# The first FFN's LayerNorm: three of its eight quarters turned by DMA, and the product behind it taken by pairs of K tiles

## The chip, the cores and the metric

One core of a Trainium2 chip runs the whole kernel in one launch. The metric is device time in microseconds; 2433.03 is the median of three runs of the kernel before (2432.76 to 2437.99).

## The reference

One layer of a streaming encoder over 256 tokens of width 2048, in float32, post-norm with `ALPHA = 2 ** 0.25`:

```python
h = layer_norm(ALPHA * h + 0.5 * swiglu_ffn(h, ffn1_w_in, ffn1_w_out), ln_ffn1_g, ln_ffn1_b)
mix = hybrid_mixer(h, w_in, ...)          # A: chunked attention, B: latent attention, both gated
h = layer_norm(ALPHA * h + mix, ...)
h = layer_norm(ALPHA * h + memory_cross_attention(h, mem, ...), ...)
h = layer_norm(ALPHA * h + 0.5 * swiglu_ffn(h, ...), ...)
# in hybrid_mixer: qa, ka, va, q_lat, kv_lat, gates = split(u @ w_in)
```

The change lies between the first `layer_norm` and the products `va` (2048 x 1024, the values of attention A) and `gates`.

## The kernel before

Weights stream from memory in blocks of 128 x 2048 (1 MB): K on the partitions, 16 K tiles of 128. Every float32 operand is split in two rounded halves, hi and lo, and a product is three matmuls: hi·hi, lo·hi and hi·lo. For weights `halves` (L258 to L268) does the split: two casts on ScalarE (L264) and one subtraction on VectorE (L267). Three raw buffers hold loaded blocks, two pairs of buffers ("units") hold the split ones; a block with tags goes to other, named buffers instead. SyncE issues the loads in order (L193); a load waits until the subtraction has released its raw buffer.

The activations are held transposed (`T`, four blocks of four K tiles, each with hi and lo for both tiles of 128 tokens). A LayerNorm therefore ends with a turning. `ln_T` (L405 to L434) takes quarters of 512 columns: it normalises one (even quarters on VectorE L413, odd ones on ScalarE L415), turns its four 128 x 128 tiles on TensorE into PSUM (L421, placed behind the last matmul in program order), applies gain and bias alternately on ScalarE (L428) and VectorE (L430), and splits the result (`split`, L254 to L257). The scale comes from `ln_scale`, a chain of some ten small VectorE operations whose last one is `self.chain`; the low halves of weights are queued behind that one.

The FFN's last output product and the next product are *skewed*: four weight blocks are kept, the first token tile goes through all four, then the second, so that a LayerNorm's turning can run beside the other tile's matmuls. Behind the FFN comes `mixer` (L869). Its first product, A's values, takes `w_va` in eight blocks of four K tiles by 512 columns: the first column half skewed over both token tiles, all 16 K tiles each, then the second half for both tiles together (`mm_tok`, L298). Into it are woven the second token tile's LayerNorm, and in its second half four `forms_step`, sums of activation tiles that the gates' products need (L321, L325). Each value result is copied from PSUM by L891. Behind it stand four gate products (`pair_group`: `mm_pair`, L311, and a seven-product scheme over sums of weights, `mm_sums`, L366), the latent product and the projections.

A scheduler orders the instructions of each engine ahead of time: by program order, moved forward by a priority (`SOON` is 400), as they become ready in its own model. `issue_after(x)` forces an instruction behind `x` on its engine.

The other way of turning exists already, for the LayerNorm before cross-attention (`turned_norm`, L1386): a quarter is normalised on VectorE (L1405), its 32-bit words are copied on ScalarE into two planes of 16 bits (L846), a transposing DMA from SyncE turns them (L850), ScalarE joins the planes again (L854), gain and bias follow from SBUF (L1426, L1428), then the split.

Of the kernel before, what the change touches and what calls it, by code (L numbers as in the profile page):

```python
# [101 lines left out]
class Kernel:  # L102
    def __init__(self, ctx, tc, t, out):
        self.tc, self.nc, self.t, self.out = tc, tc.nc, t, out

        def pool(name, bufs=1, **kw):
            return ctx.enter_context(tc.tile_pool(name=name, bufs=bufs, **kw))

        self.const = pool("const")
        self.wraw = pool("wraw", 3)  # L110
        self.whi = pool("whi", UNITS)
        self.wlo = pool("wlo", UNITS)
        self.blocks = pool("blocks")
# [8 lines left out]
        self.cut = self.early = False  # L122


# [46 lines left out]
    def weave(self, main, side, prio=SOON):  # L171

        for i in range(len(main) + 1):
            for f in side.get(i, ()):
                self.add(f, prio=prio, held=main[i][2] if i < len(main) else 0)
            if i < len(main):
                self.items.append(main[i])

    def run(self):
# [21 lines left out]
        def load(i):  # L201
# [3 lines left out]
            if isinstance(w, Sums):  # L205
                n = 4 * w.m
                got = self.halves(raw[:, w.m:n], *self.unit()), self.halves(
                    sums[i][:, :n], *(self.block(g, (P, 2048), F32R) for g in w.tags))
            else:
                ap, tags = w  # L210
                hi, lo = (self.block(g, (P, 2048), F32R) for g in tags[:2]) if tags else self.unit()
                first = {"turned": self.ln_act, "next": self.last_hi}.get(tags[2]) if tags and len(tags) > 2 else None
                with self.tc.issue_after(first.ins) if first else nullcontext():
                    got = self.halves(raw[:, :ap.shape[1]], hi, lo)
            form_sums(i + 1)
# [38 lines left out]
    def split(self, src, hi, lo):  # L254
        copied = self.nc.scalar.copy(hi, src)
        self.nc.vector.tensor_tensor(lo, src, hi.bitcast(F32), ALU.subtract)
        return copied  # L257

    def halves(self, src, hi, lo):

# [41 lines left out]

    def mm_pair(self, ps, w, n, x, kts, first, last):

        for wi in range(2):
            for j, kt in enumerate(kts):
                for tt in range(2):
                    for g in range(2):
# [97 lines left out]
    def ln_T(self, h, mr, tt, ln, xT, qs=range(4)):  # L406
# [3 lines left out]
        for q in qs:  # L410
# [349 lines left out]
    def out_proj(self, wname, nk, x, scale, st, steps=None, tags=None, n0=0, other=False, cut=False):  # L760
# [109 lines left out]
    def mixer(self, xT, st, steps):  # L870
# [4 lines left out]

        va, kept, ps1 = {}, {}, {}

        def val(n, tts, g, ps, tags=None, held=0, keep=False, again=False):
            def fn(w=None):
                if keep:  # L880
                    kept[g] = w
                w = kept.pop(g) if again else w
                for tt in tts:
                    if g == 0:
                        ps[tt] = self.mm_tile()
                    self.mm_tok(ps[tt], tt, w, xT(), range(4 * g, 4 * g + 4), g == 0, g == 3)
                if g == 3:
                    if "t" not in va:
                        va["t"] = self.block("H4", (P, 2, 1024))
                    for tt in tts:  # L890
                        (nc.vector.tensor_copy if tt else nc.scalar.copy)(  # L891
                            va["t"][:, tt, n * 512:(n + 1) * 512], ps[tt])
            ap = t["w_va"][n, :, g * 2048:(g + 1) * 2048]
            self.add(fn, *(() if again else ((ap, tags),)), held=held)

        ps = {}
        first = self.collect(lambda: self.skewed(
            lambda tt, g, **kw: val(0, (tt,), g, ps, **kw), (),
            (None, None, ("H5", "H0", "early"), ("X0", "X1", "turned"))))
        a, b, c = steps(1)  # L900
        self.weave(first, {0: a, 3: b, 4: c})
        gates, fx = {}, {}
        second = self.collect(lambda: [val(1, (0, 1), g, ps1) for g in range(4)])
        self.weave(second, {1 + i: [self.forms_step(fx, SUMS_GATE, c, xT)] for i, c in enumerate(SUMS_GATE)}, prio=0)


# [7 lines left out]
        def gate(n):  # L914
            ps, qs = {}, {}

            def product():
# [7 lines left out]
                if n < 2:  # L925
                    load_bias(n + 2)
            self.pair_group(n % 2, t["w_gate"][n], 512, KT, xT, AT_GATE[n], fx, ps, qs, None, SUM_HOME + ("H5",),
                            ORDER_GATE if len(AT_GATE[n]) > 3 else None)
# [53 lines left out]

        self.pair_group(0, t["w_lat"][0], 512, KT, xT, SUMS_IN, fx, lps, lqs, None, SUM_HOME + ("H5",))
        self.add(lat_scale, prio=SOON)
# [7 lines left out]
        def kpe(w):  # L992
# [3 lines left out]
            rope = self.rotation()  # L996
            ps = self.at_tile()
            for kt in range(KT):
# [386 lines left out]

    def turned_norm(self, ln, st, x):  # L1386

# [4 lines left out]
        def scale(tt):  # L1392
            def fn():
                if tt == 0:
                    x["T"] = self.act(["T0", "T1", "T2", "T3"])
                got[tt] = self.ln_scale(st[tt])
            return fn

        def planes(tt, q):
            def fn():  # L1400
                if tt == 0:
                    e[q] = self.block(("X2", "X3", "H5", "H4")[q], (P, 2, 2, 512))
# [14 lines left out]
        def join(tt, q):  # L1417
            def fn():
# [222 lines left out]
    def build(self):  # L1641
# [57 lines left out]
def _layout(i):  # L1699
# [22 lines left out]
    r["w_qk"] = np.stack([_feat(w[:, :aw]), _feat(w[:, aw:2 * aw])], 1)  # L1722
    r["w_va"] = _tok(w[:, 2 * aw:3 * aw])
    c = 3 * aw
# [52 lines left out]
```

## Time and profile before

| | |
|---|---|
| runs, median (lowest to highest) | 2433.03 us (2432.76 to 2437.99) |
| profiled execution, its span | 2432.52 us, 2430.7 us |
| TensorE busy | 2422.3 us, 11280 matmuls |
| VectorE busy | 2130.9 us |
| ScalarE busy | 1553.2 us |
| granted TensorE clock | 1.00 throughout |

Busy shares are of the span. Matmuls overlap in the record, so a row's length is a little over the distance from its start to the next row's start; distances between starts are the measure used. Times in rows count from the start of the span. The stretch of the change is 677 to 730 us: the FFN's last two blocks for the second token tile, the LayerNorm's turnings, A's values.

### The profile page before, as it was taken

How to read it: one execution, taken by the hardware profiler on the slowest of the kernel's cores; microseconds unless marked ns; L12 is line 12 of the kernel's file. 1: busy time of each engine (PE TensorE's matmuls, PEld its weight loads, DVE VectorE, ACT ScalarE, POOL GpSimd, SP SyncE). 2: the span in 40 equal slices, each digit the busy share in tenths (PEclk: the TensorE clock that was granted, in tenths of full speed). 3: DMA queues.
4: the chain of work that ended last, by engine and by line, in shares of the span. 5: the costliest groups of instructions: out<-in, count | busy, mean ns of one | idle time of the engine just before them, and what ended most of it. 6: DMA issues, size and time to landing. Idle time of an engine off the chain costs nothing.

```text
span 2430.7 us, 29702 instructions
## 1 busy us (share of the span) xinstructions
PE 2422.3 (100%) x11280; PEld 2022.8 (83%) x11280; DVE 2130.9 (88%) x2437; ACT 1553.2 (64%) x2022; POOL 35.9 (1%) x81
## 2 busy tenths in 40 slices
PE   9999999999999999999999999999999999999999
PEld 8888888888888888888888888888888888888887
DVE  8999989899889998779788889979879999888997
ACT  6676745666555557878565687765666675556662
POOL 0000000000000001000000000000000000000000
PEclk9999999999999999999999999999999999999999
DMA  7766656667656657776577577655556766666665
GB/s 268 252 212 214 207 200 222 210 201 219 224 176 215 216 195 248 229 210 176 183 246 256 167 241 213 220 181 192 190 199 214 229 221 210 220 207 207 200 220 182
DMA packets 176414, 516.20 MB, mean 212 GB/s; under 512 B 111728, under 2 KB 112496, under 8 KB 121104
## 3 DMA queue, kind: packets, MB, share of 16 engines
q1 hardware_dynamic: 170816, 495.83, 61.6%
q0 software_dynamic: 4592, 17.30, 2.2%
q8 instruction: 88, 1.44, 0.2%
q10 hardware_dynamic: 864, 1.18, 0.1%
q14 instruction: 54, 0.44, 0.1%
HBM read 485.30 MB, written 2.10 MB: 201 GB/s over the span
## 4 chain that ended last, share of the span: by engine, by line
PE 89%; DVE 4%; ACT 3%; DMA 1%; issue 1%; SPq 0%; DVEq 0%; ACTq 0%
PE at L311 24%; PE mm L311 23%; PE at L366 11%; PE mm L366 11%; PE mm L298 10%; PE mm L277 4%; PE mm L279 2%; DVE lo L267 2%; ACT hi L264 1%; PE at L1034 1%; PE at L1505 0%; PE at L277 0%; DMA raw<-w_xv 0%; PE at L1088 0%; ACT H L854 0%
## 5 line engine op out<-in xcount | busy, mean ns | idle before, releaser
L264 ACT CAST hi<-raw 128x1024 fp32r<-128x1024 f32 (+1 forms) x852 | 804.0, 981 | 458.0 <-PE at L311 150.1
L267 DVE TENSOR_TENSOR lo<-raw,hi 128x2048 fp32r<-128x2048 f32 (+1 forms) x427 | 902.0, 2114 | 134.8 <-ACT hi L264 129.0
L311 PE MATMUL mm<-hi,T 128*128 128x512 f32 (+1 forms) x1312 | 307.5, 384 | 0.8 <-DVE v L400 0.7
L311 PEld LDWEIGHTS mm<-hi,T 128*128 128x128 f32 x1312 | 244.5, 188 | 46.9 <-DVE v L400 1.1
L264 ACT CAST X<-H 128x1024 fp32r<-128x1024 f32 (+1 forms) x170 | 174.8, 1035 | 160.9 <-DVE H L248 119.9
L311 PE MATMUL at<-hi,T 128*128 128x512 f32 x1136 | 272.3, 390 | 0.0
L311 PEld LDWEIGHTS at<-hi,T 128*128 128x128 f32 x1136 | 213.3, 188 | 44.5
L267 DVE TENSOR_TENSOR X<-H,X 128x2048 fp32r<-128x2048 f32 (+1 forms) x85 | 191.4, 2252 | 64.7 <-ACT X L264 64.7
L311 PE MATMUL mm<-lo,T 128*128 128x512 f32 (+1 forms) x656 | 158.4, 383 | 0.0
L311 PE MATMUL at<-lo,T 128*128 128x512 f32 x568 | 141.0, 389 | 0.0
L311 PEld LDWEIGHTS mm<-lo,T 128*128 128x128 f32 x656 | 122.3, 188 | 22.4
L311 PE MATMUL at<-hi,H 128*128 128x512 f32 x560 | 133.8, 390 | 0.0
L311 PEld LDWEIGHTS at<-lo,T 128*128 128x128 f32 x568 | 106.7, 188 | 22.1
L311 PEld LDWEIGHTS at<-hi,H 128*128 128x128 f32 x560 | 105.0, 188 | 21.5
L250 DVE TENSOR_TENSOR H<-H,raw 128x512 f32<-128x512 f32 (+1 forms) x170 | 115.4, 679 | 2.2
L311 PE MATMUL mm<-hi,H 128*128 128x512 f32 x480 | 115.5, 392 | 0.1
L311 PEld LDWEIGHTS mm<-hi,H 128*128 128x128 f32 x480 | 89.6, 188 | 18.9 <-DVE w L684 0.5
L248 DVE TENSOR_TENSOR H<-raw 128x1024 f32<-128x1024 f32 (+1 forms) x85 | 102.1, 1201 | 0.6 <-DMA raw<-w_gate 0.4
L366 PE MATMUL mm<-X,X 128*128 128x512 f32 x342 | 91.4, 393 | 0.0
L264 ACT CAST X<-raw 128x1024 fp32r<-128x1024 f32 (+1 forms) x54 | 55.4, 1035 | 47.9 <-DVE raw L250 38.6
L366 PE MATMUL at<-X,X 128*128 128x512 f32 (+1 forms) x315 | 82.6, 386 | 0.7 <-ACT X L264 0.7
L854 ACT COPY w<-w 128x1024 uint16<-128x1024 uint16 (+1 forms) x60 | 75.7, 1275 | 1.4 <-DMA w<-w 1.4
(387 smaller groups left out, 4151.3 us busy)
## 6 DMA issues: line engine op xcount, KB each, us to landing
raw<-ffn_w_in SPq DMA_DIRECT2D x150, 1024.0 KB, 4.9
raw<-ffn_w_out SPq DMA_DIRECT2D x66, 1024.0 KB, 4.9
raw<-w_gate SPq DMA_DIRECT2D x32, 1024.0 KB, 4.8
raw<-ffn_w_out_r SPq DMA_DIRECT2D x16, 1024.0 KB, 4.9
raw<-w_qk SPq DMA_DIRECT2D x16, 1024.0 KB, 5.6
raw<-w_o_b SPq DMA_DIRECT2D x16, 1024.0 KB, 4.8
raw<-w_out SPq DMA_DIRECT2D x16, 1024.0 KB, 5.0
raw<-w_xk SPq DMA_DIRECT2D x16, 1024.0 KB, 5.4
```

The lines of the kernel that those rows point to most:

```text
L248: self.nc.vector.tensor_tensor(two[0], two[1], raw[:, :m].unsqueeze(1).to_broadcast([P, 2, m]), ALU.add)
L250: self.nc.vector.tensor_tensor(t[:, a * m:a * m + m], t[:, b * m:b * m + m], raw[:, a * m:a * m + m], ALU.add)
L264: self.last_hi = self.nc.scalar.copy(hi[:, c:d], src[:, c:d])
L267: self.last_lo = self.nc.vector.tensor_tensor(lo[:, :n], src, hi[:, :n].bitcast(F32), ALU.subtract)
L277: self.nc.tensor.matmul(ps, hi[j], x.both(kt), start=(j == 0), stop=False)
L279: self.last_mm = self.nc.tensor.matmul(ps[:, :S], lo[j], x.at(0, kt), start=False, stop=(j == n - 1))
L298: self.last_mm = self.nc.tensor.matmul(ps, x.at(xi, kt)[:, tt * P:(tt + 1) * P], w[wi][:, j * 512 + c:j * 512 + c + m], start=(start and j ...
L311: self.last_mm = self.nc.tensor.matmul(ps[tt, g][:, :n], x.at(xi, kt)[:, tt * P:(tt + 1) * P], w[wi][:, c:c + n], start=first and j + wi + ...
L366: self.last_mm = self.nc.tensor.matmul(bank[:, :m], a[xi], v[wi][:, c * m:(c + 1) * m], start=own and first and wi + xi == 0, stop=own and ...
L854: self.nc.scalar.copy(self.words(u, n).rearrange("p (c k) -> p k c", k=2), self.words(s, n).rearrange("p (k c) -> p k c", k=2))
L1034: nc.tensor.matmul(ps[:, c0:c0 + nk], q[:, tt * P:(tt + 1) * P], k[:, :nk], start=(j == 0), stop=(j == len(parts) - 1))
```

## The change

- For the first FFN's LayerNorm, quarters 2 and 3 of the first token tile and quarter 3 of the second are turned by DMA; the other five stay on TensorE. Their normalising is queued behind the last low half of a turned quarter (`ln_lo`), their planes copy behind its rounding (`ln_act`). The planes stand in buffers `F` and `X2`.
- A's values take `w_va` in pairs of K tiles by both column halves, into four PSUM banks: K tiles 0 to 7 skewed (first tile, then second), K tiles 8 to 15 for both tiles together. The layout in memory follows.
- The low half of the third value block (tag "after") is not queued behind the scale's chain but after the first tile's turned quarters.
- The four `forms_step` and the copies of the values stand at the end of the product; the gates', the latent and the rotary key's products exchange the PSUM banks they use.

```diff
     def ln_T(...):
             turned = self.split(v, hi, lo)
-            if q == 1:
-                self.ln_act = turned
+            if q == qs[-1]:
+                self.ln_act, self.ln_lo = turned, self.last_split
+        while self.late:
+            self.late.pop(0)(self.ln_lo)
...
-    def halves(self, src, hi, lo):
+    def halves(self, src, hi, lo, late=False):
...
-        with self.tc.issue_after(self.chain.ins) if self.chain is not None else nullcontext():
-            self.last_lo = self.nc.vector.tensor_tensor(lo[:, :n], src, hi[:, :n].bitcast(F32), ALU.subtract)
+        def low(behind=None):
+            first = behind or self.chain
+            with self.tc.issue_after(first.ins) if first is not None else nullcontext():
+                self.last_lo = self.nc.vector.tensor_tensor(lo[:, :n], src, hi[:, :n].bitcast(F32), ALU.subtract)
+        if late:
+            self.late.append(low)
+        else:
+            low()
...
+    def skewed_pairs(self, src, ps, xT, side, tags):
+        kept = {}
+        def add(k, tts, tags=None, held=0, keep=False, again=False):
+            def fn(w=None):
+                if keep:
+                    kept[k] = w
+                w = kept.pop(k) if again else w
+                if k == 0:
+                    ps.update({(tt, g): self.group_tile(0) for tt in tts for g in range(2)})
+                self.mm_pair(ps, w, 512, xT(), (2 * k, 2 * k + 1), k == 0, k == 7, tts)
+            self.add(fn, *(() if again else ((src[:, k * 2048:(k + 1) * 2048], tags),)), held=held)
+        def build():
+            self.skewed(lambda tt, k, **kw: add(k, (tt,), **kw), (), tags)
+            for k in range(4, 8):
+                add(k, (0, 1))
+        self.weave(self.collect(build), side)
...
     def mixer(self, xT, st, steps):
+        side = dict(steps(1))
+        for i, c in enumerate(SUMS_GATE):
+            side.setdefault(9 + i, []).append((self.forms_step(fx, SUMS_GATE, c, xT), 0))
+        side[12].insert(0, values)
+        self.skewed_pairs(t["w_va"][0], ps, xT, side, (None, None, ("H5", "H0", "early", "after"), ("X0", "X1", "turned")))
...
-            self.pair_group(n % 2, t["w_gate"][n], ...)
+            self.pair_group(n % 2 ^ 1, t["w_gate"][n], ...)
...
     def planes(tt, q):                      # in turned_norm
-                nc.vector.tensor_scalar(hs, hs, mean, r, ALU.subtract, ALU.mult)
-                with self.tc.issue_after(self.next_hi.ins):
+                with nullcontext() if homes[0] else self.tc.issue_after(self.ln_lo.ins):
+                    nc.vector.tensor_scalar(hs, hs, mean, r, ALU.subtract, ALU.mult)
+                with self.tc.issue_after((self.next_hi if homes[0] else self.ln_act).ins):
                     self.planes(hs, e[q][:, tt, 0, :], 512)
...
+        if not homes[0]:
+            def low(f, *a):
+                return f(*a), 0
+            side = {0: [scale(1)], 1: [low(planes, 0, 2), low(planes, 0, 3)], 2: [low(send, 0, 2)],
+                    3: [low(send, 0, 3), near(1)], 5: [near(1, (2,)), low(planes, 1, 3)],
+                    6: [low(join, 0, 2), low(send, 1, 3)], 7: [low(join, 0, 3)], 9: [low(join, 1, 3)]}
+            return lambda tt: side if tt else ([scale(0)], [near(0)], [])
...
-        ln = [self.ln_steps(n, st, x) for n in ("ln_ffn1", "ln_mix", "ln_x")]
+        ln = [self.turned_norm("ln_ffn1", st, x, (None, None, "F", "X2")), None, self.ln_steps("ln_x", st, x)]
```

The keys of `side` are places in the product of A's values: 0 to 3 are the first tile's K tile pairs 0 to 3, 4 to 7 the second tile's, 8 to 11 the pairs 4 to 7 for both.

## Rows read from the trace of the kernel before

**Rows 1.** The page: busy us, share of the span and instructions of each engine.

```profile
PE 2422.3 (100%) x11280; PEld 2022.8 (83%) x11280; DVE 2130.9 (88%) x2437; ACT 1553.2 (64%) x2022; POOL 35.9 (1%) x81
```

**Rows 2.** Stretches: start and end, length, busy us of each engine, granted clock, DMA.

```profile
677.40:729.70 52.30, 52.30 (x247) 43.24 (x246) 44.48 (x88) 31.85 (x52) 1.23 (x2) 1.00 0.43 150
...
707.90:729.70 21.80, 21.80 (x98) 18.03 (x97) 16.84 (x24) 11.03 (x16) 1.23 (x2) 1.00 0.61 212
729.70:771.00 41.30, 41.30 (x184) 34.23 (x183) 36.35 (x30) 23.74 (x28) 0.00 (x0) 1.00 0.63 225
```

**Rows 3.** Waits of PE: line, releaser, us in total, times, longest.

```profile
PE at L493 <- DVE w L470: 1.1, 1, 1.1
```

**Rows 4.** Timeline of PE: start, us, line, operation, out<-in, count.

```profile
677.41 2.88 PE L298 MATMUL mm<-X,H 128*128 128x512 f32 x12
680.27 1.06 PE L421 MATMUL at<-ident,h 128*128 128x128 f32 x8
681.09 2.32 PE L298 MATMUL mm<-X,H 128*128 128x512 f32 x9
683.25 1.03 PE L421 MATMUL at<-ident,h 128*128 128x128 f32 x8
684.04 2.28 PE L298 MATMUL mm<-hi,T 128*128 128x512 f32 x8
...
693.31 3.01 PE L298 MATMUL mm<-X,T 128*128 128x512 f32 x12
...
707.93 1.98 PE L298 MATMUL mm<-hi,T 128*128 128x512 f32 x8
...
729.69 3.79 PE L311 MATMUL mm<-hi,T 128*128 128x512 f32 x16
```

**Rows 5.** Timeline of DVE, same columns; in brackets idle time before and its releaser.

```profile
675.01 2.27 DVE L267 TENSOR_TENSOR H<-raw,H 128x2048 fp32r<-128x2048 f32 x1
677.20 0.26 DVE L395 BATCH_NORM_AGGREGATE mv<-bn 128x2 f32<-128x24 f32 x1
...
683.68 0.69 DVE L256 TENSOR_TENSOR T<-w,T 128x512 fp32r<-128x512 f32 x1 [0.34 <-ACT T L255]
...
707.89 0.29 DVE L325 TENSOR_TENSOR w<-w 128x128 f32<-128x128 f32 x1
...
727.78 2.28 DVE L267 TENSOR_TENSOR X<-H,X 128x2048 fp32r<-128x2048 f32 x1
```

**Rows 6.** Timeline of ACT.

```profile
701.07 2.96 ACT L264 CAST hi<-raw 128x1024 fp32r<-128x1024 f32 x3
```

**Rows 7.** Timeline of SP, the loads of w_va.

```profile
673.80 0.33 SPq L193 DMA_DIRECT2D raw<-w_va  x1
...
677.32 0.33 SPq L193 DMA_DIRECT2D raw<-w_va  x1
...
693.78 0.33 SPq L193 DMA_DIRECT2D raw<-w_va  x1
```

**Rows 8.** Instructions on tile H, 1375 to 1440 us: ns min/median/max, first, last start.

```profile
L1426 ACT ACTIVATE H<-H,vecs x8: 478/493/513, 1420.6 to 1433.7; 128x128 f32<-128x128 f32 x8
L846 ACT COPY H<-h x4: 1042/1060/1063, 1399.2 to 1417.2; 128x1024 uint16<-128x1024 uint16 x4
...
L854 ACT COPY H<-H x4: 1346/1354/1381, 1418.2 to 1428.9; 128x1024 uint16<-128x1024 uint16 x4
L255 ACT CAST T<-H x4: 609/614/638, 1421.6 to 1435.0; 128x512 fp32r<-128x512 f32 x4
...
DMA to landing us min/median/max: 3.0/3.5/4.2
```

**Rows 9.** Line L850, all transposing DMAs.

```profile
DMA to landing us min/median/max: 2.7/3.2/12.9
```

**Rows 10.** Timeline of PE beside the turnings before cross-attention.

```profile
1396.18 3.92 PE L277 MATMUL mm<-H,hi 128*128 128x512 f32 x16 [0.28 <-ACT hi L264]
```

**Rows 11.** Chain that ended last, 1375 to 1440 us: start, us, what.

```profile
1389.39 5.67 DMA raw<-w_xk
```

More of the change, by code (lines that the diff above doesn't have):

```diff
@@ L122, in __init__ @@
         self.cut = self.early = False
+        self.late = []
     def name(self, s):
@@ L174, in weave @@
             for f in side.get(i, ()):
-                self.add(f, prio=prio, held=main[i][2] if i < len(main) else 0)
+                f, p = f if isinstance(f, tuple) else (f, prio)
+                self.add(f, prio=p, held=main[i][2] if i < len(main) else 0)
             if i < len(main):
@@ L213, in load @@
                 with self.tc.issue_after(first.ins) if first else nullcontext():
-                    got = self.halves(raw[:, :ap.shape[1]], hi, lo)
+                    got = self.halves(raw[:, :ap.shape[1]], hi, lo, bool(tags) and "after" in tags)
             form_sums(i + 1)
@@ L301, in mm_tok, with mm_pair @@
                     )
-    def mm_pair(self, ps, w, n, x, kts, first, last):
+    def mm_pair(self, ps, w, n, x, kts, first, last, tts=(0, 1)):
         for wi in range(2):
             for j, kt in enumerate(kts):
-                for tt in range(2):
+                for tt in tts:
                     for g in range(2):
@@ L873, in mixer, with values @@
         e = self.__dict__
[L876 to L904, printed above, removed]
+        va, ps, gates, fx = {}, {}, {}, {}
+        def values():
+            va["t"] = self.block("H4", (P, 2, 1024))
+            for n in range(2):
+                for tt in range(2):
+                    (nc.vector.tensor_copy if tt else nc.scalar.copy)(
+                        va["t"][:, tt, n * 512:(n + 1) * 512], ps[tt, n])
+        side = dict(steps(1))
[3 more added lines that the diff above has]
+        self.skewed_pairs(t["w_va"][0], ps, xT, side, (None, None, ("H5", "H0", "early", "after"), ("X0", "X1", "turned")))
         bias = {}
@@ L926, in product @@
                     load_bias(n + 2)
-            self.pair_group(n % 2, t["w_gate"][n], 512, KT, xT, AT_GATE[n], fx, ps, qs, None, SUM_HOME + ("H5",),
+            self.pair_group(n % 2 ^ 1, t["w_gate"][n], 512, KT, xT, AT_GATE[n], fx, ps, qs, None, SUM_HOME + ("H5",),
                             ORDER_GATE if len(AT_GATE[n]) > 3 else None)
@@ L981, in lat_join @@
             return fn
-        self.pair_group(0, t["w_lat"][0], 512, KT, xT, SUMS_IN, fx, lps, lqs, None, SUM_HOME + ("H5",))
+        self.pair_group(1, t["w_lat"][0], 512, KT, xT, SUMS_IN, fx, lps, lqs, None, SUM_HOME + ("H5",))
         self.add(lat_scale, prio=SOON)
@@ L996, in kpe @@
             rope = self.rotation()
-            ps = self.at_tile()
+            ps = self.mm_tile()
             for kt in range(KT):
@@ L1384, in mem_norm, with turned_norm @@
         return {0: [load], 2: [stat(0)], 6: [stat(1)], 8: [spread], 9: [quarter(0)], 11: [quarter(1)], 13: [quarter(2)], 14: [quarter(3)]}
-    def turned_norm(self, ln, st, x):
+    def turned_norm(self, ln, st, x, homes=("X2", "X3", "H5", "H4")):
         nc, e, got = self.nc, {}, {}
@@ L1393, in fn @@
             def fn():
-                if tt == 0:
+                if tt == 0 and homes[0]:
                     x["T"] = self.act(["T0", "T1", "T2", "T3"])
@@ L1397, in scale, with near, fn @@
             return fn
+        def near(tt, qs=(0, 1)):
+            def fn():
+                if tt == 0:
+                    x["T"] = self.act(["T0", "T1", "T2", "T3"])
+                self.ln_T(self.h[tt], got[tt], tt, ln, x["T"], qs)
+            return fn
         def planes(tt, q):
             def fn():
-                if tt == 0:
-                    e[q] = self.block(("X2", "X3", "H5", "H4")[q], (P, 2, 2, 512))
+                if q not in e:
+                    e[q] = self.block(homes[q], (P, 2, 2, 512))
                 mean, r, nb = got[tt]
                 hs = self.h[tt][:, q * 512:(q + 1) * 512]
-                nc.vector.tensor_scalar(hs, hs, mean, r, ALU.subtract, ALU.mult)
-                with self.tc.issue_after(self.next_hi.ins):
+                with nullcontext() if homes[0] else self.tc.issue_after(self.ln_lo.ins):
+                    nc.vector.tensor_scalar(hs, hs, mean, r, ALU.subtract, ALU.mult)
+                with self.tc.issue_after((self.next_hi if homes[0] else self.ln_act).ins):
                     self.planes(hs, e[q][:, tt, 0, :], 512)
@@ L1722, in _layout @@
     r["w_qk"] = np.stack([_feat(w[:, :aw]), _feat(w[:, aw:2 * aw])], 1)
-    r["w_va"] = _tok(w[:, 2 * aw:3 * aw])
+    r["w_va"] = _pairs(*_halves(w[:, 2 * aw:3 * aw]), 512, [()])
     c = 3 * aw
```

2 lines of the change are left out of this document (1 added, 1 removed).

## The prediction

> **What bounds it.** Read in this order: the busy shares, the stretch of the change, TensorE's waits, then the engines' timelines around the first FFN's LayerNorm. TensorE is busy 2422.3 of 2430.7 us [rows 1], in the changed stretch 52.30 of 52.30 at a granted clock of 1.00, which is 2.4 GHz [rows 2]; its longest wait for another engine in the whole span is 1.1 us, at the start [rows 3]. So the time is a sum of matmuls, and a change can win only what it takes off TensorE and the small gaps between its instructions. The reader is to see this in the timeline: from 707.93 to 729.69 stand 96 matmuls of 512 columns, 0.2267 us each, without a gap [rows 4]. VectorE is second, 44.48 of 52.30 us here and 36.35 of 41.30 in the first gate group behind it [rows 2].
>
> **What leaves TensorE.** Eight turnings take from 680.27 to 681.09 and from 683.25 to 684.04: 0.82 and 0.79 us, 0.10 each [rows 4]. Three of eight quarters at four turnings each no longer run there: 12 x 0.10 = 1.2 us. The product A's values keeps its 192 matmuls (16 K tiles x 3 passes x 2 token tiles x 2 column halves, in another order).
>
> **Entries.** The 12 matmuls from 677.41 end at 680.13, the turnings start at 680.27; the nine from 681.09 end at 683.13, the next start at 683.25: about 0.13 us a group [rows 4]. Four groups become three (two of eight, one of four): 0.13 us.
>
> **The low half out of the chain.** VectorE rounds `lo` of the third weight block from 675.01 for 2.27 us, and the aggregate of the first token tile starts behind it at 677.20 [rows 5]. Moved behind the turned quarters, it lets the chain of small operations start about 2.1 us earlier. The turnings still stand behind TensorE's matmuls, which end at 680.13, so only the 0.14 us of waiting before the first of them can go. The price is that this raw buffer comes free later: the load at 677.32 is the one it releases [rows 7]. The casts of this block and the one before it run only from 701.07 on [rows 6], so some 10 us of slack (a load at 688, landed by 695) hide it.
>
> **Cover lost.** Today eight turnings of the second half stand between the last FFN matmuls and the first value matmuls, while the first quarter is evacuated, scaled and split. Its low half is written at 683.68 + 0.69 = 684.37 [rows 5], 4.1 us after the turnings began; even so the first eight value matmuls took 2.28 us against 1.98 in later rows, 0.3 us of waiting [rows 4]. Afterwards TensorE reaches them at 680.13 + 0.80 + 9 x 0.2267 = 682.97 and wants the first low half 0.23 later, at 683.2. At today's pace it would come at 680.13 + 4.1 = 684.2, a wait of 1.0; if ScalarE, which has one normalisation less in front, and the earlier chain bring it 0.7 sooner, 0.3. I take 0.7, nearest to the row's own pace, 0.4 more than today. For the second token tile 12 matmuls (2.72) still stand behind the turnings, as at 693.31 [rows 4], so 3.5 us cover a chain of some 3.8: 0.05 more than today.
>
> **Sum.** -1.2 - 0.13 - 0.14 + 0.4 + 0.05 = -1.0 us. The profiled execution took 2432.52 us (span 2430.7, 1.8 around it); the median of the runs is 2433.03, 0.5 above. Against the median: 2432.0 us.
>
> **What is added beside TensorE.** Each turned quarter has on ScalarE a planes copy of 1.06 us, a joining copy of 1.35 and two scalings of 0.49, and on SyncE a transposing DMA landing 3.5 us after its issue, 4.2 at most here [rows 8], 12.9 at most anywhere [rows 9]. Three times the two copies is 7.2 us more ScalarE work, less the PSUM reads that were there anyway; ScalarE is busy 31.85 of 52.30 [rows 2], so I cost it at nothing while it is in time. VectorE normalises the odd quarters too, about 1 us more.
>
> Whether it is in time is the open cost. First token tile, third quarter: ordered behind the low half of quarter two (about 685), then perhaps behind the postponed 2.27, so normalised by about 688, copied to planes by 689, landed by about 693. The join then stands on ScalarE behind the next weight's cast, which needs a high buffer that TensorE frees only after the second tile's first eight matmuls, about 698: the cast of 2.0 us ends near 701. The join and what follows it (1.35 + 2 x 0.49 + 0.61 [rows 8] + 0.69 [rows 5] = 3.6) end at 704.6 if the join goes next. TensorE wants it where it takes up both tiles at once, which is 707.93 today [rows 4] and about 706.9 after. A margin of 2.3 us: cost 0. If two casts of the following weight (2.0) and the last quarter's planes (1.06) go before the join, it is 707.7: 0.8 late. With the slow landing 12.9 nothing changes until the landing passes 701. Ends: 0 and about +5; I take 0 because the nearest rows, the same kind of turning before cross-attention, show one wait of 0.28 us [rows 10].
>
> The four sum forms move from beside the second half of the values to behind it: each a sum and a split of 0.69 us and four of 0.29 [rows 5], 2.5 us of VectorE, 10 in all, some 6 us of it now later than today, in a stretch with 21.80 - 16.84 = 5 us free [rows 2]. What doesn't fit slides into the first gate, whose first summed weight is rounded at 727.78 for 2.28 and used at 737 to 739, 7 to 9 us of slack [rows 5]. Cost 0, ends 0 and +3. The exchange of PSUM banks only swaps which four are in use; the four values copies must end within the 5.44 us of the first gate pair. Cost 0.
>
> **A rule that speaks against it.** By rows a turned tile costs TensorE 0.10 us, and by DMA some 7 us of latency over three engines [rows 4, 8]. The Trainium skill, "VectorE: DVE Perf Modes", section "Rules for kernel authors", says of a 128x128 transpose: "Use TensorE if PSUM dest is OK; xbar DMA otherwise". Its section "The three transpose paths" gives 390 ns against 1309 (bf16); by those figures the move would lose, which is what the first rival makes of it. On a TensorE that is always busy the row's 0.10 us is what counts.
>
> **Rivals.**
> 1. A turned quarter comes late (slower than before). Place: the first matmul on K tiles 8 and 9, or 12 and 13 for the last quarter, which is planed only near 704, landed at 709, and joined at 713.5 against a need at 717. Price: the wait itself, 1 to 5 us; it decides from 1.0 us of waiting on. At 2.5 us: 2434.5. For it: ScalarE has in the 9 us before that place two pairs of casts (4.0), a planes copy (1.06), the second tile's third quarter (1.5) and the first join (2.9), 9.5 in all; against it: the margins above.
> 2. VectorE's backlog reaches the gates: forms and joins (+5 us of work) against 5 us free; a wait of 1.5 us: 2433.5. Against it: 7 to 9 us of slack.
> 3. Weight loads queue behind the DMA turnings on SyncE. Today the fifth block is loaded at 673.80 and the seventh at 693.78 [rows 7]; after, the fifth waits for two sends (about 690) and the seventh for the third (about 706), lands at 712, and its low half is wanted at 718.4. The row for it: a wait of 0.28 us [rows 10] behind a late load that stands 5.67 us in the chain [rows 11]. At 2 us: 2434.0.
> 4. All waits of the stretch go: 52.30 - 213 x 0.2267 - 20 x 0.10 = 2.0 us won: 2431.0. That would need the first low half on time.
>
> **Numbers.** Forecast 0.45 (its own range 2431.3 to 2433.0); rivals 0.20, 0.12, 0.08, 0.15 in order. 0.2% is 4.9 us, about what can be told from no change: 2428.2 and 2437.9 bound it. Beyond the first only a reordering elsewhere could reach, 0.05; beyond the second the tails of rivals 1 and 3 and a reordering, 0.10; within 0.85. The range 2429.8 to 2436.2 takes rival 4 with some room and rivals 1 to 3 to a wait of 4 us.
>
> **What would show it.** In the changed profile: 20 turnings before 710; the aggregate near 675 and the moved low half after the first turned quarters; the joins ending before 707 and 717; TensorE's waits in this stretch under 1 us for T; the first gate pair 1.0 us earlier against the FFN's last matmuls. It is wrong if TensorE waits for a joined quarter or a cast for over 1 us, or if the difference lies outside this stretch.

## The result and the profile after

The changed kernel takes 2444.15 us (median of 6 runs, 2442.55 to 2446.89) against 2435.89 (2432.76 to 2439.24) of the kernel before beside it: ratio 1.0038, 95% interval 1.0028 to 1.0048. The forecast was 2432.0 with a range of 2429.8 to 2436.2: wrong, on the slow side. The profiled execution took 2444.11 us, span 2442.3.

The page of the changed kernel, busy us of each engine, which answers to [rows 1]: TensorE has its 12 turnings less, and is busy for longer all the same.

```profile
PE 2425.0 (99%) x11268; PEld 2019.8 (83%) x11268; DVE 2131.8 (87%) x2439; ACT 1558.9 (64%) x2026; POOL 36.0 (1%) x81
```

The stretches of [rows 2] in the changed kernel (length, busy us of PE, PEld, DVE, ACT and POOL, granted clock, DMA share, GB/s), and its waits of TensorE, against [rows 3]. In 52.30 us TensorE is idle for 4.04, its clock falls short of 1.00, and a wait of 3.6 us for a cast stands at the head of the list, where 1.1 us at the start, which is still there, was the longest before.

```profile
677.40:729.70 52.30, 48.26 (x210) 37.98 (x209) 36.90 (x71) 33.08 (x50) 1.23 (x2) 0.97 0.49 149
707.90:729.70 21.80, 18.24 (x73) 14.25 (x72) 13.72 (x30) 12.16 (x19) 1.23 (x2) 0.92 0.77 236
```

```profile
PE mm L319 <- ACT hi L266: 3.6, 1, 3.6
PE mm L285 <- ACT hi L266: 1.5, 1, 1.5
PE mm L319 <- DVE v L408: 1.1, 1, 1.1
```

TensorE's timeline of the changed kernel, against [rows 4] (start, us, line, operation, out<-in, count, in brackets idle before and its releaser):

```profile
679.88 1.03 PE L429 MATMUL at<-ident,h 128*128 128x128 f32 x8
680.67 2.30 PE L306 MATMUL mm<-X,H 128*128 128x512 f32 x9
683.06 2.38 PE L319 MATMUL mm<-hi,T 128*128 128x512 f32 x8
...
692.43 3.01 PE L319 MATMUL mm<-X,T 128*128 128x512 f32 x12
695.84 2.38 PE L319 MATMUL mm<-hi,T 128*128 128x512 f32 x8 [0.39 <-ACT T L257]
...
713.38 3.79 PE L319 MATMUL mm<-hi,T 128*128 128x512 f32 x16
717.01 1.97 PE L319 MATMUL mm<-lo,T 128*128 128x512 f32 x8
722.54 5.30 PE L319 MATMUL mm<-hi,T 128*128 128x512 f32 x16 [3.56 <-ACT hi L266]
```

The reader is to see three things. The turnings start 0.39 us earlier; 0.26 of it lies ahead of them, in the start of the 12 matmuls before them (677.15 against 677.41). Block 6 ends at 718.98 and TensorE then stands still for 3.56 us, since block 7 of A's values has not been cast. And the 16 matmuls behind the gap take 5.30 us where the 16 at 713.38 took 3.79. The windows of the changed kernel show why:

```profile
712.00:718.00 6.00, 6.00 (x28) 4.96 (x27) 0.31 (x2) 0.00 (x0) 0.00 (x0) 1.00 1.07 188
718.00:722.00 4.00, 0.98 (x5) 0.48 (x3) 1.75 (x5) 3.77 (x6) 0.00 (x0) 1.00 1.02 426
722.00:726.00 4.00, 3.46 (x9) 2.79 (x10) 3.93 (x7) 3.89 (x6) 0.00 (x0) 0.57 0.72 297
```

Behind the gap the granted clock is 0.57 over 4 us, for most of them the lower of its two levels, 1.2 GHz. So the gap costs 3.56 and another 5.30 - 3.79 = 1.51 us of half clock: 5.07. In the first window ScalarE does nothing for 6 us, and VectorE next to nothing (0.31). What they wait for stands in ScalarE's timeline, then SyncE's, then POOL's, then the DMA issues of 705 to 730 (count, KB each, median us from issue to landing), all of the changed kernel:

```profile
707.48 1.05 ACT L876 COPY X<-h 128x1024 uint16<-128x1024 uint16 x1
...
718.19 1.34 ACT L884 COPY X<-X 128x1024 uint16<-128x1024 uint16 x1 [8.10 <-DMA X<-X]
719.56 0.88 ACT L1447 ACTIVATE X<-X,vecs 128x128 f32<-128x128 f32 x2
720.40 0.62 ACT L257 CAST X<-w 128x512 fp32r<-128x512 f32 x1
720.92 0.61 ACT L257 CAST T<-X 128x512 fp32r<-128x512 f32 x1
721.44 1.99 ACT L266 CAST hi<-raw 128x1024 fp32r<-128x1024 f32 x2
```

```profile
708.55 1.23 SPq L880 DMA_TRANSPOSE X<-X  x1
709.87 1.32 SPq L195 DMA_DIRECT2D raw<-w_va  x2
```

```profile
708.09 1.23 POOL L925 DMA_DIRECT2D X<-gate_row  x2 [705.83 <-PE mm L319]
```

```profile
raw<-w_gate SPq DMA_DIRECT2D x3, 1024.0 KB, 4.9
raw<-w_va SPq DMA_DIRECT2D x2, 1024.0 KB, 11.6
X<-gate_row POOLq DMA_DIRECT2D x2, 512.0 KB, 6.9
X<-X SPq DMA_TRANSPOSE x1, 9.6
```

The third quarter is copied to planes at 707.48 and its transposition sent at 708.55, between the two loads of gate bias on POOL's queue (708.09 and 708.79, 512 KB each). It takes 9.6 us. On ScalarE its join waits 8.10 us, with the cast of block 7 behind it in the queue; and blocks 7 and 8 could only be sent at 709.87, behind the transposition on SyncE (block 7 at 693.78 before [rows 7]). The first two transpositions, sent at 689.41 and 690.69, took 3.2 us each, and nothing waited for them.

Where the 11.6 us between the two profiled spans lie, read by the start of the same matmul in both traces: -0.2 at the FFN's last blocks (677.41 before), +5.2 at the first gate (729.69), +6.7 at 808, +6.4 at 1285, +9.7 at 1522, +10.6 at the last matmul, +11.6 at the end of the span. From the FFN's last 12 matmuls to the first gate the kernel before takes 52.3 us (677.41 to 729.69), the changed one 57.8 (677.15 to 734.93).

### The profile page after: what moved, and what is told of

The parts are those of the page before. It is cut to its first block, busy times and chain, and to the rows that moved or that the text cites. A ratio compares the mean times of both kernels' runs of the same rounds, so it can differ in the third digit from the quotient of the medians.

```text
span 2442.3 us, 29692 instructions
## 1 busy us (share of the span) xinstructions
PE 2425.0 (99%) x11268; PEld 2019.8 (83%) x11268; DVE 2131.8 (87%) x2439; ACT 1558.9 (64%) x2026; POOL 36.0 (1%) x81
## 4 chain that ended last, share of the span: by engine, by line
PE 88%; DVE 5%; ACT 3%; DMA 2%; issue 2%; SPq 0%; DVEq 0%; ACTq 0%
PE at L319 25%; PE mm L319 22%; PE mm L374 11%; PE at L374 11%; PE mm L306 9%; PE mm L285 5%; PE mm L287 2%; ACT hi L266 1%; DVE lo L271 1%; PE at L1047 1%; DMA raw<-w_xq 1%; DMA raw<-ffn_w_in 1%; PE at L1533 0%; PE at L1101 0%; PE at L285 0%
## 5 line engine op out<-in xcount | busy, mean ns | idle before, releaser
L319 PE MATMUL mm<-hi,T 128*128 128x512 f32 (+1 forms) x1328 | 314.5, 385 | 5.4 <-ACT hi L266 3.6
L319 PE MATMUL at<-hi,T 128*128 128x512 f32 x1216 | 291.2, 389 | 0.0
L319 PEld LDWEIGHTS at<-hi,T 128*128 128x128 f32 x1216 | 228.2, 188 | 47.8
L319 PE MATMUL at<-lo,T 128*128 128x512 f32 x608 | 150.3, 389 | 0.0
L319 PEld LDWEIGHTS at<-lo,T 128*128 128x128 f32 x608 | 114.1, 188 | 23.7
L374 PEld LDWEIGHTS mm<-X,X 128*128 128x128 f32 x360 | 66.8, 188 | 15.9 <-DVE X L271 2.2
```

Of the source, the lines that this page charges most:

```text
L319: self.last_mm = self.nc.tensor.matmul(ps[tt, g][:, :n], x.at(xi, kt)[:, tt * P:(tt + 1) * P], w[wi][:, c:c + n], start=first and j + wi + ...
L374: self.last_mm = self.nc.tensor.matmul(bank[:, :m], a[xi], v[wi][:, c * m:(c + 1) * m], start=own and first and wi + xi == 0, stop=own and ...
```

## Experiments

Each kernel is compared with runs of the kernel before on the same chip: e1 to e4 with 2434.74 us (25 runs), e5 to e8 with 2434.31 (22), e9 to e11 with 2434.10 (19), e12 and e13 with 2433.70 (15). The theory from these rows: the third transposition is late, it holds back the loads behind it on SyncE, and the join holds back the cast. Rivals: the banks, the moved low half, VectorE's backlog.

**e1_two_dma.** The third quarter goes back to TensorE.

```
-  5: [near(1, (2,)), low(planes, 1, 3)], 6: [low(join, 0, 2), low(send, 1, 3)], ... 9: [low(join, 1, 3)]
+  5: [near(1, (2, 3))],                  6: [low(join, 0, 2)],                  ... 9: []
```

> The changed kernel with the third DMA quarter (second token tile, quarter 3) turned on TensorE again; the first tile's two stay on DMA. Theory Q (SyncE's queue: the seventh and eighth value blocks wait behind the third send, go out at 709.87 instead of 693.78 and 704.48, and land 11 to 13 us later in a crowd): the two loads go out near 693 and 704 again, TensorE's waits of 3.56 + 1.5 us before the seventh block vanish, four turnings come back (+0.4): 4.5 to 6 us less than the changed kernel, about 2438. Theory J (any joined quarter comes late, the first tile's too): only part of it goes, a wait stays at the fifth block. Theory D (the loss lies in VectorE's work moved to the gates): under 2 us less.

Measured: 2436.61, ratio 1.0008 [0.9999, 1.0017]. No wait of TensorE over 0.4 us between 600 and 1000. The third quarter is the loss.

**e2_free_loads.** The weight loads are no longer held behind the third send.

```
-  self.sent = self.send(v[:, 1, :], v[:, 0, :], 512)
+  put = self.send(v[:, 1, :], v[:, 0, :], 512)
+  if homes[0] or tt == 0:
+      self.sent = put
```

> The changed kernel with three DMA quarters, but the third send no longer holds the loads that follow it in program order (the order kept behind it is dropped), so on SyncE the value blocks seven and eight stand before it. Theory Q: those loads go out near 694 and 703, land in 5 us, the wait at the seventh block falls from 5.1 us to under 1 us: 4 to 5 us less than the changed kernel. Theory J (the third quarter's planes, ready at 708.5, are late by themselves; its turning lands near 713, joined at 717): a wait of 1 to 3 us stays, on T and not on a cast.

Measured: 2445.94, ratio 1.0049 [1.0034, 1.0064]: no faster than the changed kernel. The theory as it stood falls. Block 7 is now cast in time, but the transposition, sent at 710.61, takes 14.8 us beside two gate loads (708.47 and 718.16) and the bias rows. ScalarE's, then TensorE's timeline of this kernel:

```profile
713.81 2.00 ACT L266 CAST hi<-raw 128x1024 fp32r<-128x1024 f32 x2 [1.66 <-PE mm L319]
725.50 1.33 ACT L884 COPY X<-X 128x1024 uint16<-128x1024 uint16 x1 [9.69 <-DMA X<-X]
```

```profile
728.79 5.79 PE L319 MATMUL mm<-hi,T 128*128 128x512 f32 x12 [6.85 <-ACT T L257]
```

Its window from 714 to 722, when the transposition and the second bias row are in flight, and behind 716.8 nothing else on the two queues but a gate load sent at 718.2: the DMA engines are counted busy at 1.29 and move 121 GB/s.

```profile
714.00:722.00 8.00, 7.93 (x35) 6.22 (x34) 2.95 (x4) 1.81 (x2) 0.00 (x0) 1.00 1.29 121
```

**e3_early_third.** The third quarter's planes and send one step sooner.

```
-  5: [near(1, (2,)), low(planes, 1, 3)], 6: [low(join, 0, 2), low(send, 1, 3)]
+  4: [low(planes, 1, 3)], 5: [near(1, (2,)), low(send, 1, 3)], 6: [low(join, 0, 2)]
```

> The changed kernel with the third quarter's planes made one place earlier (behind the second tile's first two turned quarters instead of behind its third), sent near 699 instead of 708.55, still in front of the sixth to eighth value loads. Theory Q: loads out at 700 to 705, no crowd with the bias rows at 708, wait at the seventh block under 1 us: 4 to 6 us less than the changed kernel. Theory C (a transposing DMA in front of the loads costs by itself some 7 us of latency wherever it stands): 2 us or less is won, and the sixth block's cast waits instead.

Measured: 2435.98, ratio 1.0006 [0.9996, 1.0015]. Sent at 698.74, the transposition lands 3.1 us later, before the bias rows begin (708.16). The DMA issues of this kernel from 696 to 705:

```profile
raw<-w_va SPq DMA_DIRECT2D x3, 1024.0 KB, 6.7
X<-X SPq DMA_TRANSPOSE x1, 3.1
```

**e4_pairs_only.** All eight quarters on TensorE; pairs, low half and banks stay.

```
-  side = {0: [scale(1)], 1: [low(planes, 0, 2), low(planes, 0, 3)], 2: [low(send, 0, 2)], ...
+  side = {0: [scale(1)], 1: [near(0, (2, 3))], 3: [near(1)], 5: [near(1, (2, 3))], 9: []}
```

> The changed kernel's product by pairs of K tiles, its bank exchange and its postponed low half, but all eight quarters turned on TensorE (32 turnings): the first tile's quarters 2 and 3 at its second block, the second tile's at its sixth place. Theory Q: no send, loads early, no wait over 1 us: 1.2 us of turnings more than e1 less its waits, 4 to 5 us less than the changed kernel. Theory D (forms behind the product, exchange of banks): it stays within 3 us of the changed kernel.

Measured: 2436.11, ratio 1.0007 [0.9998, 1.0016]. No quarter goes by DMA here, and the time is that of e1 and e3: two quarters by DMA, or three in time, win nothing that can be told in the medians. Inside the traces the places differ: from the FFN's last 12 matmuls to the first gate e4 takes 54.0 us (676.97 to 730.98) and e3 52.2 (677.23 to 729.45), so that three quarters off TensorE win 1.8 us in their own stretch. What takes them back stands further on, at e12 and e13.

**e5_late_rows and e6_free_late_rows.** The bias rows were to go behind the values, by an order given to the planner alone; e5 on the changed kernel, e6 on e2.

```
-  self.add(lambda: [load_bias(n) for n in range(2)])
+  def rows():
+      with self.tc.issue_after(va["last"].ins):
+          for n in range(2):
+              load_bias(n)
+  self.add(rows)
```

> The changed kernel with one edit: the two gate-bias rows (512 KB each, on POOL's queue) are sent only after the copies of A's values, past the projection, so they are out of the stretch 708 to 718 in which the third quarter's transposition is under way. Theory R (the rows crowd the transposition): it lands about 3 to 5 us after its issue at 708.5 instead of 9.6, its join stands at about 712, block 7 of the values is cast at about 716 instead of 721.4, PE's wait at 722.5 falls from 3.56 to under 1, and the time is 2438 to 2441. Theory L (the 1 MB weight loads issued right behind it crowd it, the rows are no part): it lands 8 us or more after its issue, PE still waits over 2.5 us there, and the time stays at 2443 to 2446. Theory S (the weight loads held on SyncE behind the third send): the loads still start at 709.9 and their landing alone, about 5 us sooner without the rows' megabyte, decides: PE waits about 1 us, time about 2441.

> The kernel of e2_free_loads (weight loads not held behind the third send) with the gate-bias rows sent past the projection as in e5. In e2 the transposition took 14.8 us and its join came at 725.5. Theory R (the rows): it lands within 5 us, at about 715, the join is in time for PE's need near 717, PE waits under 1 us in the seventh and eighth blocks, and the time is 2435 to 2438, below e5. Theory L (the 1 MB gate loads): the transposition still takes 8 us or more behind the gate load issued at 708.5, PE waits 3 us or more there, and the time is 2441 or more.

Measured: 2443.78, ratio 1.0035 [1.0021, 1.0049], and 2444.09, ratio 1.0034 [1.0020, 1.0047]. The edit did not move the rows behind the values: they are sent from 708.58 and 709.14 on (708.09 in the changed kernel, 710.16 in e2), and the transposition takes 9.9 and 12.9 us. So these two decide nothing between the theories; they are second runs of the changed kernel and of e2, with the same result.

**e9_rows_behind and e10_free_rows_behind.** The same two kernels, the rows held by data: a column of A's values is first written into their home.

```
+  bias["t"] = self.block("X1", (P, 2, 1024))
+  nc.vector.tensor_copy(bias["t"][:, 0, 0:1], va["t"][:, 1, 1023:1024])
+  nc.vector.tensor_copy(bias["t"][:, 1, 0:1], va["t"][:, 1, 1023:1024])
   for n in range(2):
       load_bias(n)
```

> The changed kernel with the two gate-bias rows really held: two one-column VectorE copies from A's values into the rows' home stand ahead of their loads, so the rows cannot start before the values are copied out, past 735 (in e5 and e6 the edit did not move them, they were still issued at 708.6 and 709.1). Theory R (transposition and bias rows slow each other): the third transposition, issued near 708.5, lands 3 to 6 us later instead of 9.6, its join stands near 713, block 7's load (issued at 709.9) lands by about 716, PE's wait at block 7 falls from 3.6 to under 1 and the clock stays at 1.00; time 2436 to 2439. Theory L (the three 1 MB weight loads behind it slow it): it still takes 8 us or more, PE waits over 2.5 us, and the time stays at 2443 to 2446.

> The kernel of e2_free_loads (weight loads not held behind the third send) with the bias rows held as in e9. In e2 the transposition took 14.8 us beside one gate load and the second bias row. Theory R: it lands within 6 us (near 715), the join is no later than 716, PE waits under 1 us in blocks 7 and 8; time 2435 to 2438. Theory L: it takes 8 us or more beside the 1 MB gate load; PE waits 3 us or more; time 2441 to 2446.

Measured: e9 2437.54, ratio 1.0016 [1.0006, 1.0025]; e10 2435.43, ratio 1.0004 [0.9995, 1.0013]. The rows now start at 737.83 and 734.01. ScalarE's timeline of e9, TensorE's of e9, e9's window against the one of the changed kernel above, then e9's DMA issues from 705 to 730 and e10's:

```profile
713.12 1.35 ACT L884 COPY X<-X 128x1024 uint16<-128x1024 uint16 x1 [3.15 <-DMA X<-X]
...
717.81 2.00 ACT L266 CAST hi<-raw 128x1024 fp32r<-128x1024 f32 x2 [1.32 <-DMA raw<-w_va]
```

```profile
718.91 3.94 PE L319 MATMUL mm<-hi,T 128*128 128x512 f32 x16
```

```profile
712.00:718.00 6.00, 6.00 (x28) 4.96 (x27) 2.96 (x7) 3.52 (x6) 0.00 (x0) 1.00 0.96 381
```

```profile
raw<-w_gate SPq DMA_DIRECT2D x3, 1024.0 KB, 4.6
raw<-w_va SPq DMA_DIRECT2D x2, 1024.0 KB, 8.9
X<-X SPq DMA_TRANSPOSE x1, 4.6
```

```profile
X<-X SPq DMA_TRANSPOSE x1, 5.0
```

Theory R holds, theory L falls: sent at the same moment and with the same three megabytes of weights behind it, the transposition takes 4.6 us instead of 9.6, TensorE waits nowhere for block 7, and the clock stays at 1.00 (from 722 to 726 too, where the changed kernel had 0.57). With the changed kernel and e2 this is a square, in median us:

| | bias rows at 708 | bias rows behind the values |
|---|---|---|
| loads held behind the third send | 2444.15 | 2437.54 |
| loads free | 2445.94 | 2435.43 |

The rows' meeting with the transposition is worth 6.6 us in one line and 10.5 in the other. The runs of the kernel before beside the four differ, though (2435.89 and 2434.74 on the left, 2434.10 on the right); taken as distances from them the two lines give 4.8 and 9.9. Holding the loads costs 2.1 us, and only where the transposition is quick. e9 is still told from the kernel before, e10 is not.

**e7_early_low_in.** e3 with the low half of the third value block (tag "after"; the expectation calls it the fourth) back in its chain.

```
-  ("H5", "H0", "early", "after")
+  ("H5", "H0", "early")
```

> The kernel of e3_early_third (third quarter's transposition sent one step sooner) with the low half of the fourth values block cast back into its chain, as the kernel before had it. What remains of the change: A's values in K-tile pairs, three quarters by DMA planes, and the exchange of banks. If taking the low half out of its chain delays the second tile's normalisation (PE's wait of 0.4 us before its first matmul at about 695.9, aggregate behind the postponed subtraction), that wait is gone and the time is 0.3 to 0.5 below e3's 2436.0, but PE waits about 0.1 again before the first tile's first turning at 680. If the low half's place costs nothing at the second tile, the time is the same as e3's within 0.2 and the 0.4 us wait stands.

Measured: 2435.98, ratio 1.0007 [0.9998, 1.0016]. The wait at the second tile is gone: VectorE's aggregate starts at 685.99 instead of 687.65, and TensorE's timeline shows 0.12 us between the 12 matmuls' end (692.56 + 12 x 0.2267 = 695.28) and the next, and 2.16 for the eight:

```profile
692.56 3.01 PE L319 MATMUL mm<-X,T 128*128 128x512 f32 x12
695.40 2.16 PE L319 MATMUL mm<-hi,T 128*128 128x512 f32 x8
```

The mechanism is shown, but little of its 0.8 us is left at the first gate (52.2 us from the FFN's last 12 matmuls in e3 and in e7), and nothing can be told in the medians. The other half of the expectation was a miss: no wait came back ahead of the first turning (the 12 matmuls before it end at 677.24 + 12 x 0.2267 = 679.96, it starts at 679.97).

**e8_banks_only.** The kernel before with the banks exchanged.

```
-  self.pair_group(n % 2, t["w_gate"][n], ...      (and 0, at_tile() for the latent and the rotated key)
+  self.pair_group(n % 2 ^ 1, t["w_gate"][n], ...  (and 1, mm_tile())
```

> The kernel before with one part of the change alone: the banks of the gates', the latent's and the rotated key's sums exchanged. The prediction took this as 0. If the 1.5 us that the changed kernel loses at the start of the first gate come from the banks, the first gate's waits after 771 appear here too and the time is 1 to 2 us above before; if they come from VectorE's backlog behind the late third quarter, PE's waits stand as before and the time is within 0.1% of before.

Measured: 2433.73, ratio 1.0000 [0.9992, 1.0009]. From 600 to 1000 its trace has one wait, 2.1 us ahead of the turnings at 682.15, where no bank is exchanged yet, and none at the gates. The banks cost nothing. That wait, and the clock behind it (0.60 from 682 to 686, nine matmuls in 3.72 us where e12 takes 2.31), belong to this execution, which took 2438.24.

**e11_late_join.** The changed kernel with the third join one step later.

```
-  9: [low(join, 1, 3)]
+  10: [low(join, 1, 3)]
```

> The changed kernel with the third quarter's join one step later, so that on ScalarE it stands behind the cast of block 7 and TensorE may take the first tile's matmuls of blocks 7 and 8 while the second tile's quarter is missing. If ScalarE's order (the cast queued behind a join that waits for a DMA) is the main price, PE's wait at block 7 falls to the load's own lateness (landing 720.6 + 1.2 for the cast, a wait of about 2.5 instead of 3.6) and the time falls by 1 to 2 us, to 2442 to 2443. If the lateness of the transposition and of block 7's load decides, whichever comes first on ScalarE, the time stays within 1 us of the changed kernel's 2444.

Measured: 2448.90, ratio 1.0063 [1.0048, 1.0078]: worse, a miss for both. The cast now stands ahead of the join, and starts at 720.57, as block 7 lands; but the planner gave TensorE the first tile's matmuls first, in small groups with a wait before each. TensorE's timeline:

```profile
721.66 3.08 PE L319 MATMUL mm<-hi,T 128*128 128x512 f32 x8 [2.87 <-ACT hi L266]
724.94 0.79 PE L319 MATMUL mm<-lo,T 128*128 128x512 f32 x1 [0.19 <-DVE lo L271]
727.32 1.22 PE L319 MATMUL mm<-hi,T 128*128 128x512 f32 x2 [1.59 <-ACT T L257]
```

ScalarE's order is worth 0.7 us of the first wait (2.87 against 3.56). What lies under it is the two landings.

**e12_before_again and e13_free_rows_low_in.** The kernel before for a second trace, and e10 with e7's edit: every cause found removed.

> The kernel before, unchanged, for a second trace of it. In its first trace the cross-attention stretch (about 1285 to 1522) took 236.8 us with 1.0 us of TensorE waits over 0.15 us; in the traces of the repaired variants (e3, e7, e10), whose instructions past the projections stand in the same order, it took 239.6 to 240.1 with 2.8 to 3.1 us. If that is variation between executions, this trace takes 238 to 240 there. If the change alters that stretch in some way, this trace takes 236.8 within 0.5 again.

> All repairs at once: weight loads not held behind the third send, the gate-bias rows held until A's values are copied out, and the fourth block's low half back in its chain. What remains of the change: pairs, three quarters by DMA planes, banks. If the causes found are all there is, no wait of TensorE over 0.15 us is left between 680 and 1000, the twelve turnings saved (1.2 us) stand at the first gate as a start 0.3 to 0.9 us earlier than before's 729.7, and the time is 2433.5 to 2435.5, not told from before. If the change has a cost that is not found yet, the time is above 2436.

Measured: e12 one run of 2433.25; its cross-attention stretch took 238.5 us, with 2.0 of waits, against 236.8 in the first trace: the rows ahead of the prediction come from one of the quicker executions, and up to 1.7 of the 3.3 us that the changed kernel loses there may be variation. All kept traces together say more: the stretch takes 236.8 to 238.5 us in the four without added transpositions (the kernel before, e12, e8, e4) and 239.3 to 241.8 in the eleven with two or three of them, 2.2 apart in the mean, though from 945 us of the kernel before on every engine has the same instructions in the same order. The eight transpositions `w<-H` of that stretch land in 4.4 to 4.5 us (median) in the four and in 4.8 to 5.3 in the eleven. From the DMA issues from 1285 to 1530, of the kernel before and of e13:

```profile
w<-H SPq DMA_TRANSPOSE x8, 4.4
```

```profile
w<-H SPq DMA_TRANSPOSE x8, 5.1
```

So a part of the loss there goes with the added transpositions, some 600 us behind them; by what way is not shown. e13 took 2435.61, ratio 1.0008 [0.9999, 1.0017]. Its list of TensorE's waits is empty from 600 to 1000, and the first gate's matmuls start at 728.91, 0.78 us before [rows 4]. But e12 is there at 728.92, and from the FFN's last 12 matmuls to the gate both take 51.9 us (from 677.01 and 677.00):

```profile
728.91 3.79 PE L319 MATMUL at<-hi,T 128*128 128x512 f32 x16
```

The stretch was as expected, the time a little above it. Two things are left. One is the end of the span: the last two matmuls start at 2426.31 of 2432.7 us here, at 2435.82 of 2442.3 in the changed kernel, but at 2425.99 of 2431.5 in e12 and 2427.51 of 2433.0 in e4. TensorE's last rows, of e13 and e4:

```profile
2426.31 1.02 PE L1653 MATMUL mm<-T,w 128*128 128x512 f32 x2
```

```profile
2427.51 1.02 PE L1643 MATMUL mm<-T,w 128*128 128x512 f32 x2
```

That is 6.4 to 6.5 us with three added transpositions and 5.5 without any: 0.9 to 1.0 us. The other is cross-attention, 239.4 us in e13, 0.9 to 2.6 above the four traces without added transpositions.

## Why the prediction was wrong

- **What leaves TensorE, entries:** right in the count, 20 turnings stand before 710; the gain in time is not shown. From the FFN's last 12 matmuls to the first gate e13, without the losses, takes 51.9 us, 0.4 less than the first trace of the kernel before and no less than e12, against 1.0 in the sum. By the prediction's own count (213 x 0.2267, 0.10 a turning) the small waits of that stretch are 1.6 us in e13, 0.8 in the first trace and 0.4 in e12: what the turnings leave goes into waits for cover.
- **Cover lost, first tile:** right. The first eight value matmuls start 0.35 us behind the nine before them (680.67 + 9 x 0.2267 = 682.71) and take 0.40 more than 1.98: 0.75 against the 0.7 taken.
- **The low half out of the chain, and cover lost at the second tile:** the 0.14 us ahead of the first turning is gone, but it was not the low half's: e12 and e7, with the low half in its chain, have no such wait either (677.00 + 12 x 0.2267 = 679.72, start 679.73 in e12). And the step priced only the buffer, and the postponed 2.27 us stand at 685.46 ahead of the second tile's aggregate: 0.69 before the eight matmuls and 0.40 in them, 1.09 against the 0.05 + 0.1 taken; e7 takes most of it away.
- **What is added beside TensorE: this step failed.** "First token tile, third quarter" was worked through and was right: joins at 700.51 and 705.26, no wait. For the second tile's quarter, the last, cost 0 was carried over from it. Its planes copy began at 707.48 and ended at 708.53, not near 704, because ScalarE and VectorE took two casts, two low halves and the first tile's joins before them; and the landing was taken as about 5 us where 9.6 came, within the 12.9 of [rows 9] that the text set aside for the first tile. The price was 3.56 of waiting and 1.51 of low clock, 5.07, which is the +5 taken as the far end, and 1.5 more at the first gate.
- **Rivals 1 and 3** were one case, not two: the same late send delays the quarter and, on SyncE, the weights. Each alone was priced at 2 to 2.5 us. The text had the send at 706 (measured 708.55) and block 7 landed at 712 (720.60). What was missing is the neighbour, which the prediction never looked at: the bias rows, in the same stretch in the trace of before, too. Its DMA issues from 700 to 725:

```profile
X<-gate_row POOLq DMA_DIRECT2D x2, 512.0 KB, 6.1
```

The trace of before also had such a meeting: the 12.9 of [rows 9] is a transposition sent at 1258.0, behind a load of `mem` that POOL sent at 1253.77. DMA issues from 1250 to 1262 in the kernel before:

```profile
T<-mem POOLq DMA_DIRECT2D x1, 1024.0 KB, 7.0
H<-H SPq DMA_TRANSPOSE x4, 9.9
```

Two weight loads were in flight there as well, so this row shows where the slow landings stood, not by itself what made them slow.

- **Rival 2:** the 1.5 us at the first gate are real (739 to 808), but come from the held loads, not from forms: in e10, with the same forms and free loads, nothing is lost there; in e9, with held loads, 1.6.
- **Banks:** 0, as taken (e8).

What the Trainium skill says of transposes, in "VectorE: DVE Perf Modes", section "Rules for kernel authors" (TensorE where a result in PSUM will do), holds for the whole kernel: e4, with all quarters on TensorE, is not told from the best variants with transposing DMAs. In the stretch itself it does not (54.0 us in e4 against 52.2 in e3); the DMA's price is in its landing, in cross-attention and at the end of the span.

## What to carry to other kernels

A transfer that moves into a new place is priced by what is in flight at that place on every queue, not by its median landing elsewhere: list what is in flight there before giving it a margin. Work through the last of several like items, not the first; it has the least slack and the longest queue ahead. A wait of 3.6 us on a TensorE that was busy all along cost 1.5 us more in clock. And the changed stretch is not the whole price: of the 11.6 us here 3.3 lie in cross-attention and 1.0 at the end of the span.

## What the runs showed of the hardware

- A transposing DMA of 256 KB landed in 3.0 to 3.3 us with nothing of another queue beside it (in e3 with two 1 MB weight loads sent 1.3 and 2.0 us behind it), in 4.6 to 5.2 in e9, e10 and e13, where what made it slower is open, and in 9.6 to 14.8 with the two bias rows in flight on POOL's queue. The second row landed in 8.9 us in the changed kernel and in 14.9 in e2; with no transposition beside them rows took 4.3 to 7.8 (5.2 the second in e3, 7.8 in e1). The DMA share read over 1 while the bytes moved fell to 121 GB/s; the same engines moved 381 GB/s from 712 to 718 in e9. Packets of each queue (count, MB, share of 16 engines), in the changed kernel from 708.5 to 711.8, where POOL's is the only queue with any, then of SyncE's queue in e9 from 708.5 to 713:

```profile
q0 software_dynamic: 102, 0.42, 35.2%
```

```profile
q1 hardware_dynamic: 1086, 0.51, 84.6%
```

  The transposition of the changed kernel, sent at 708.55, has no packet before 711.8; from then to 718 SyncE's queue has 1088 and POOL's 186. The Trainium skill, "DMA: Bandwidth & Descriptors", section "Queues, rings and completion order", says that a DMA engine takes turns between the queues it has work for, packet by packet. The trace agrees in so far as both queues have packets from 711.8 to 718; the 3 us before, with none on SyncE's, stay open, and whether the rows' form (one row into 128 partitions) or their queue matters was not tried.
- After 3.56 us without a matmul the granted clock was 0.57 over the next 4 us; after 6.85 us in e2 it was 0.50 from 726 to 732, and 12 matmuls took 5.79 us. In e8, after 2.10 us of waiting ahead of eight turnings, it was 0.60 from 682 to 686. In e9, with no gap, it stayed at 1.00.
- The end of the span grew with added transpositions that had landed 1700 us before: from the last two matmuls' start to the end 5.5 us without added transpositions, 6.4 to 6.5 with three; from the last matmul's end it is 4.5 in e4, 5.1 in e1 with two, and 5.3 to 5.5 in e3, e7 and e13 with three. More than 3 us behind the last matmul SyncE has 12 to 13 events and drains in e1, e3 and the changed kernel against 7 in the kernel before and e4. Why was not tried.
